# The start-up of a matmul, mask and softmax kernel: mask loaded ahead of W, fills shared among engines, TensorE run on zeros, and W four rows to a partition

## Chip, cores and metric

One core of one Trainium2 chip. The metric is device time in microseconds (us) of one execution; lower is better. "Span" is the same execution as the profile sees it, 1.7 to 2.5 us less than the measured time, by kernel. Each run carries a state. For one core, a run is called slow when it is over 1.5% above the fastest run of the same kernel, and ratios use the fast runs alone. That label matters in this case and is discussed with the result.

## The reference

```
y = scale * matmul(x, weight)          # x: 16 x 512 x 512, weight: 512 x 512, scale 0.125
y = where(mask == 1, y, -1e9)          # mask: lower triangle of 512 x 512
out = softmax(y, axis=-1)              # float32, 16 x 512 x 512
```

Traffic is 16.8 MB of x in, 16.8 MB of out, 1 MB of W and 0.26 MB of mask (only its four diagonal blocks are read).

## The kernel before

The kernel works on sixteen tiles u, each of half the rows of two batch entries, four rows of x to a partition, 1 MB in and 1 MB out. For a tile: one load, a cast to bf16 on VectorE, sixteen PE transposes, eviction of the transposes by VectorE and ScalarE, matmuls plus one "band" matmul that adds the mask, exp with row sums on ScalarE, reciprocal and scaling on VectorE, one store. Loads and stores are all issued by SyncE. Its start-up:

```python
    load(0)
    seq(nc.sync.dma_start(w_f32, weight.rearrange("(kt p) n -> p kt n", p=P)))
    seq(nc.sync.dma_start(diag_f32, diag_r))            # the mask's diagonal blocks
    for u in range(1, X_BUFS):                          # X_BUFS = 8
        load(u)
    make_identity(nc, ident_bf)
    nc.gpsimd.memset(spread, 0.0)
    # ... eight gpsimd.affine_select that build spread ...
    nc.gpsimd.memset(band[:HP, :, :, P:], MASK_NEG)
    nc.gpsimd.memset(band[HP:, :, :, :P], 0.0)
    for i in range(0, OUT_BUFS, 2):
        nc.gpsimd.memset(ots[i][:, :, HB:], 0.0)        # four wide fills
        nc.gpsimd.memset(ots[i][0:2, 0, HB:], 1.0 / N)
    cast(0); transpose(0); evict(0)
    # ... four casts of W, 128x512 each, VectorE and ScalarE in turn ...
    # ... mask to bf16 on VectorE; four matmuls spread x mask; copies into band ...
    cast(1)

    for u in range(U + 1):                              # U = 16, guards cut
        transpose(u + 1)
        cast(u + 2)
        evict(u + 1)
        multiply(u)
        normalise(u - 1); store(u - 1)
        load(u - 1 + X_BUFS)                            # only after a store is issued
```

The last line matters: after the first eight, a load is issued only behind a store. Until the first store the DMA queue holds eight x tiles, W and the mask and nothing else.

The softmax here doesn't subtract the row's maximum and nothing guards it: scores larger than these inputs give would overflow.

## Time and profile before

| | before |
|---|---|
| time, median of the first runs | 93.98 us (93.84 to 94.58, 4 runs) |
| span of the profiled run | 92.3 us (a run of 94.61 us, labelled slow) |
| bytes moved | 34.87 MB on SyncE's queue |
| first store issued | 25.63 us |
| last store issued / last byte landed | 84.57 / 91.3 us |

Two things are to be read beside the lines that the prediction shows. First, when stores are issued: the timeline of the DMA-issuing engine (start, length, engine, line, operation, what it writes and reads, count).

```profile
2.64 6.99 SPq L78 DMA_DIRECT2D xf<-in_x_dram  x7
25.63 0.61 SPq L158 DMA_DIRECT2D out_dram<-ot  x1
26.29 0.60 SPq L78 DMA_DIRECT2D xf<-in_x_dram  x1
30.77 0.60 SPq L158 DMA_DIRECT2D out_dram<-ot  x1
```

From 10 to 25.6 us nothing new enters the queue. Second, why the first store is so late: VectorE's timeline ahead of it.

```profile
5.82 2.06 DVE L83 CAST xb<-xf 128x2048 bf16<-128x2048 f32 x1 [5.82 <-DMA xf<-in_x_dram]
9.00 0.69 DVE L102 COPY xt<-pt 128x1024 bf16<-128x1024 bf16 x1 [1.13 <-PE pt L92]
9.61 3.15 DVE L193 CAST w_bf<-w_f 128x512 bf16<-128x512 f32 x2
12.68 0.61 DVE L197 TENSOR_SCALAR diag_bf<-diag_f 128x512 bf16<-128x512 f32 x1
13.96 1.70 DVE L216 CAST band<-py 64x256 bf16<-64x256 f32 x4 [0.68 <-PE py L209]
15.59 2.34 DVE L83 CAST xb<-xf 128x2048 bf16<-128x2048 f32 x2
```

A cast that takes 1.22 us later takes 2.06 here, and two W casts take 3.15 where one of them alone took 0.61. GpSimd is filling until 13.0 us. cast(1) begins near 15.6 (the first of the last row's two), 2.7 us after x(1) has landed (12.9 in the landing records).

### The profile page before, as it was taken

Reading aid. Unit: us, or ns where it says so; the run is one execution under the profiler, and the core shown is the slowest. Engines: PE = TensorE matmul, PEld = TensorE weight load, DVE = VectorE, ACT = ScalarE, POOL = GpSimd, SP = SyncE. Lnnn points to the kernel's source line nnn. Section 1 sums busy time; section 2 is a strip of 40 time slices with the busy share of each in tenths; the row PEclk is TensorE's granted clock in tenths of the full one; section 3 lists DMA queues with packets and bytes.
Section 4 is the critical chain, followed back from the end, with each engine's and each line's share of the span. In section 5 each row is a group of like instructions: output and inputs, shape, how many; then the busy total and the mean of one; then the engine's idle time right before and its main releaser. Section 6 shows DMA issues by size and latency. Waiting matters only on the chain.

```text
span 92.3 us, 1608 instructions
## 1 busy us (share of the span) xinstructions
PE 68.8 (75%) x580; PEld 48.7 (53%) x580; DVE 60.0 (65%) x119; ACT 54.4 (59%) x151; POOL 15.9 (17%) x33
## 2 busy tenths in 40 slices
PE   0005225699999999999999999999999999940000
PEld 0005100677659857956975885796598577510000
DVE  0045979950857995995999599599395977616000
ACT  5000716064868777977877788797787879650000
POOL 7999960000100010010001001000100010100000
PEclk9999999999999999999999999999999999997555
DMA  0889999999999999999999999999999999999930
GB/s 32 334 309 309 387 430 423 437 415 430 419 419 312 405 426 291 323 423 415 415 433 426 423 430 412 430 419 433 423 430 426 423 423 433 423 426 423 394 156 11
DMA packets 5670, 34.95 MB, mean 379 GB/s; under 512 B 544, under 2 KB 1056, under 8 KB 1568
## 3 DMA queue, kind: packets, MB, share of 16 engines
q1 hardware_dynamic: 5664, 34.87, 92.7%
q8 instruction: 4, 0.07, 0.3%
q14 instruction: 2, 0.02, 0.0%
HBM read 18.09 MB, written 16.78 MB: 378 GB/s over the span
## 4 chain that ended last, share of the span: by engine, by line
PE 72%; DVE 12%; DMA 5%; ACT 1%; DVEq 0%; issue 0%; ACTq 0%
PE py L116 47%; PE pt L92 17%; PE py L125 8%; DMA xf<-in_x_dram 5%; DVE xb L83 3%; DVE w_bf L193 3%; DVE band L216 2%; DVE ot L152 1%; DVE xt L102 1%; PE py L209 1%; ACT ot L135 1%; DVE diag_bf L197 1%; DVEq L263 0%; DVE rinv L150 0%; ACTq L263 0%
## 5 line engine op out<-in xcount | busy, mean ns | idle before, releaser
L116 PE MATMUL py<-w_bf,xt 128*128 128x256 bf16 (+1 forms) x256 | 51.4, 335 | 0.0
L135 ACT ACTIVATE ot<-py 128x256 f32<-128x256 f32 (+1 forms) x64 | 31.2, 493 | 9.3 <-PE py L125 9.1
L116 PEld LDWEIGHTS <-xt 128*128 128x128 bf16 x256 | 25.3, 101 | 12.6
L83 DVE CAST xb<-xf 128x2048 bf16<-128x2048 f32 x16 | 20.2, 1270 | 8.5 <-DMA xf<-in_x_dram 8.5
L92 PE MATMUL pt<-ident_bf,xb 128*128 128x128 bf16 x256 | 18.6, 231 | 9.6 <-DVE xb L83 9.6
L103 ACT COPY xt<-pt 128x1024 bf16<-128x1024 bf16 x16 | 16.2, 1012 | 15.5 <-PE pt L92 11.2
L152 DVE TENSOR_SCALAR ot<-ot,rinv 128x256 f32<-128x256 f32 (+1 forms) x64 | 23.5, 430 | 0.8
L92 PEld LDWEIGHTS <-xb 128*128 128x128 bf16 x256 | 17.0, 104 | 11.6 <-DVE xb L83 10.5
L102 DVE COPY xt<-pt 128x1024 bf16<-128x1024 bf16 x16 | 11.0, 689 | 11.3 <-PE pt L92 11.3
L125 PE MATMUL py<-band,ident_bf 128*128 128x256 bf16 x64 | 18.0, 282 | 0.0
L154 POOL MEMSET ot<- 2x256 f32 x8 | 3.6, 449 | 63.1 <-DVE ot L152 63.1
L135 ACT ACTIVATION_READ_ACCUMULATOR ot<-py 128x1 f32 x64 | 12.8, 200 | 0.0
L125 PEld LDWEIGHTS <-ident_bf 128*128 128x128 bf16 x64 | 6.5, 101 | 4.3
L150 DVE RECIPROCAL rinv<-rsum 128x4 f32<-128x4 f32 x16 | 2.7, 169 | 3.2 <-ACT ot L135 3.2
L185 POOL MEMSET ot<- 128x1024 f32 x4 | 4.6, 1185 | 0.1
L209 PE MATMUL py<-diag_bf,spread 128*128 128x512 bf16 x4 | 1.9, 620 | 3.5 <-DVE diag_bf L197 3.5
L173 POOL TENSOR_SCALAR_AFFINE_SELECT spread<-spread 128x64 bf16<-128x64 bf16 x8 | 3.2, 438 | 0.0
L193 DVE CAST w_bf<-w_f 128x512 bf16<-128x512 f32 x2 | 3.1, 1612 | 0.0
L216 ACT CAST band<-py 64x256 bf16<-64x256 f32 x4 | 1.5, 368 | 2.7 <-DVE band L216 2.5
L209 PEld LDWEIGHTS <-spread 128*128 128x128 bf16 x4 | 0.5, 136 | 4.2 <-POOL ot L186 3.7
L216 DVE CAST band<-py 64x256 bf16<-64x256 f32 x4 | 1.7, 416 | 0.7 <-PE py L209 0.7
L103 ACT ACT_TABLE_LOAD x1 | 1.3, 1283 | 0.7 <-PEq L249 0.7
(12 smaller groups left out, 6.8 us busy)
## 6 DMA issues: line engine op xcount, KB each, us to landing
xf<-in_x_dram SPq DMA_DIRECT2D x16, 1024.0 KB, 14.1
out_dram<-ot SPq DMA_DIRECT2D x16, 1024.0 KB, 11.0
w_f<-in_weight_dram SPq DMA_DIRECT2D x1, 1024.0 KB, 7.6
diag_f<-in_mask_dram SPq DMA_DIRECT2D x1, 256.0 KB, 8.3
```

Source lines behind the costliest of these rows:

```text
L83: seq(nc.vector.tensor_copy(xb, st_x.pop(u)))
L92: nc.tensor.transpose(st_pt[u][kt // 2][:, kt % 2, t], xb[:, t, kt * P : (kt + 1) * P], ident_bf,)
L102: seq(nc.vector.tensor_copy(xt[:, 0:2], pt[0]))
L103: seq(nc.scalar.copy(xt[:, 2:4], pt[1]))
L116: nc.tensor.matmul(py[:, :NC], lhsT=xt[:, kt, t], rhs=w_bf[:, kt, :NC], start=(kt == 0), stop=(kt == KT - 1),)
L125: nc.tensor.matmul(py[:, h * HB : NC], lhsT=ident_bf, rhs=band[:, h, t], start=False, stop=True, skip_group_check=True,)
L135: nc.scalar.activation(out=ot[:, t, :NC], in_=py[:, :NC], func=AF.Exp, bias=0.0, scale=float(scale), accum_out=rsum[:, t : t + 1],)
L152: seq(nc.vector.tensor_scalar_mul(ot[:, t, :NC], ot[:, t, :NC], rinv[:, t : t + 1]))
L154: seq(nc.gpsimd.memset(ot[0:2, 0, :HB], 1.0 / N))
L185: nc.gpsimd.memset(ots[i][:, :, HB:], 0.0)
L193: seq(nc.vector.tensor_copy(w_bf[:, kt], w_f32[:, kt]))
L216: seq(copy(band[half, :, t, g * P : (g + 1) * P], src[half, :, g]))
```

## The change

The intent is a shorter start-up. Cut to its core:

```diff
-    seq(nc.sync.dma_start(w_f32, weight.rearrange("(kt p) n -> p kt n", p=P)))
     seq(nc.sync.dma_start(diag_f32, diag_r))
+    seq(nc.sync.dma_start(w_f32, weight.rearrange("(p kt) n -> p kt n", kt=KT)))
@@ transpose(u)
-                        xb[:, t, kt * P : (kt + 1) * P],
+                        xb[:, t].rearrange("p (k kt) -> p kt k", kt=KT)[:, kt],
@@ ahead of make_identity
+    nc.vector.memset(zeros, 0.0)
+    idle = psum_y.tile([P, N], FP32, name="py")
+    for _ in range(WARM):                       # WARM = 12
+        seq(nc.tensor.matmul(idle, lhsT=zeros[:, :P], rhs=zeros, start=True, stop=True))
@@ fills
-    nc.gpsimd.memset(spread, 0.0)               # and eight affine_select, cut
-        nc.gpsimd.memset(ots[i][:, :, HB:], 0.0)
+        nc.vector.memset(ots[i][:, :, HB:], 0.0)
+    # spread: four nc.scalar.copy out of ident_bf, cut
@@ order on the engines
     cast(0)
-    transpose(0); evict(0); four casts of W; mask to bf16; band
+    mask to bf16; transpose(0); evict(0); band; two casts of W (128x1024 each)
     cast(1)
```

The pseudo-lines of the last part stand for the moved blocks. W's rows now lie four to a partition, in runs of 8 KB, so the transposes take every fourth column of x, a step of four bf16 elements.

## The prediction

> **What bounds the kernel now.** I read the page first, then the chain of waits, the windows view, the waits of the DMA-issuing queue and the timeline of VectorE. The page offers TensorE as the bound: it holds 72% of the chain that ended last. In time order that chain shows no TensorE gap from 16.85 to 81.9 us. But the page's slices show the DMA engines at 90% or more from the second slice almost to the end, so I asked for stretches. The windows view (columns: stretch and its length; busy time and count of PE, PEld, DVE, ACT, POOL; granted clock; DMA share; GB/s):
>
> ```profile
> 2.20:5.20 3.00, 0.00 (x0) 0.00 (x0) 0.00 (x0) 0.00 (x0) 3.00 (x8) 1.00 0.92 353
> 5.20:10.20 5.00, 1.89 (x16) 1.73 (x17) 3.26 (x3) 0.34 (x1) 4.89 (x7) 1.00 0.87 308
> 10.20:27.00 16.80, 12.02 (x73) 7.71 (x73) 12.02 (x18) 8.60 (x22) 3.25 (x5) 1.00 1.01 425
> ...
> 28.00:32.00 4.00, 4.00 (x50) 3.54 (x48) 3.71 (x8) 3.27 (x12) 0.00 (x0) 1.00 0.99 350
> ...
> 35.00:39.00 4.00, 4.00 (x49) 3.53 (x48) 2.85 (x8) 3.45 (x12) 0.00 (x0) 1.00 0.90 285
> 39.00:85.00 46.00, 42.90 (x375) 29.91 (x372) 35.22 (x79) 34.35 (x100) 2.69 (x6) 0.99 1.01 425
> ...
> 88.50:91.30 2.80, 0.00 (x0) 0.00 (x0) 0.00 (x0) 0.00 (x0) 0.00 (x0) 0.50 0.10 44
> ```
>
> Look at the last column. 425 GB/s is the ceiling: both long stretches sit on it. The queue's 34.87 MB at 425 GB/s need 82.0 us, and the first packet moves at 2.2 us, so no order of the compute can land the last byte before about 84.2 us. It lands near 91.3. The 7 us between are the stretches below 425, each costing length x (1 - rate/425): 0.5 us in 2.2-5.2, 1.4 in 5.2-10.2, 0.7 in 28-32, 1.3 in 35-39, some 0.4 in 85-88.5, and 2.5 in the tail after 88.5, where 44 GB/s is one or two of 16 engines finishing late.
>
> Why the rate falls: I counted bytes issued against bytes moved in the packet records. The eight loads, W and the mask run out at 27 us, when 0.07 MB is left. The first store is issued at 25.63 and needs about 1.6 us to begin, the second at 30.77, when little is left again. From 41 us the backlog is 1.5 to 5 MB, and it is down to 0.14 MB at 86. So the DMA queue bounds the kernel, and compute matters only where it feeds stores too late: around 27-32 us and at the very end. VectorE's timeline shows the other direction, loads arriving late for compute:
>
> ```profile
> 66.79 1.23 DVE L83 CAST xb<-xf 128x2048 bf16<-128x2048 f32 x1 [1.43 <-DMA xf<-in_x_dram]
> ...
> 71.64 1.23 DVE L83 CAST xb<-xf 128x2048 bf16<-128x2048 f32 x1 [1.23 <-DMA xf<-in_x_dram]
> ```
>
> The bracket is idle time before the row and what ended it. The last two x tiles are already late for VectorE, so moving the whole compute chain earlier cannot move its end by the same amount.
>
> **What the Trainium skill says.** "DMA: Bandwidth & Descriptors", Specifications, puts the fabric ceiling at 435 GB/s; the 425 above agrees within 3%. "TensorE: Matmul & The Clock Gate", Part 1, says that matmuls start at half clock until about 3.4 us of sustained work. The trace agrees in form: sixteen transposes take 1.89 us at 16.85 but 0.89 at 22.99. The granted-clock column shows 1.00 in both places, so here I trust durations. "SBUF — State Buffer", the cacheline note in the port-swizzle section (Door 1), says steps up to 8 bf16 elements read at full rate; the new transposes step by 4. No run yet shows a strided weight load. The same page, Who interferes with whom, says a GpSimd instruction and a two-port VectorE one exclude each other; the trace agrees: the first cast, beside GpSimd fills, took 2.06 us, the median of its kind is 1.22.
>
> **The change, part by part.**
>
> 1. W at four rows to a partition: 512 packets of 2 KB become 128 of 8 KB. Packet records give medians of 84 and 309 ns: 512 x 84 / 16 = 2.69 us against 128 x 309 / 16 = 2.47. It saves 0.2 us of DMA time, and I grant 0.3 more because W's packets started with a gap (DMA share 0.58 at 5-6 us).
>
> 2. Fills. GpSimd loses 0.53 + 3.2 us for the spread matrix and 4.6 for the wide fills (4 x 1185 ns). VectorE takes the wide fills; it has no such row yet, so I use GpSimd's 1.2 us each, 4.8 in all, inside its idle 5.8 us before x(0) lands. ScalarE builds spread in four small copies, also while idle. None is on the path. GpSimd should be done before the first cast, which then takes 1.22 instead of 2.06: 0.8 us earlier.
>
> 3. Mask before W. Before, W's cast (3.1 us on VectorE, one piece slowed to 2.6 by GpSimd) stood ahead of the mask's 0.6 us, and the band matmuls waited for it until 13.34. Now: cast(0) 5.8 to 7.0, mask landed near 7.1 and converted by 7.8, eviction 0.7, four band copies of 0.42 us by about 10.5. W lands about 9.5; its cast (twice 0.61 us, nobody interfering) ends near 11.8. Then cast(1) waits for x(1), which landed at 12.9 in the records and should at 12.4-12.6. It ends near 13.8 instead of 16.80. Transposes(1) start **2.9 us earlier**, and that is set by a load.
>
> 4. Zeros on TensorE: twelve matmuls of 512 columns at 427 ns (half clock, the page's name) make 5.1 us from about 1.1, off the path. They may warm the clock for transposes(0). TensorE then idles from about 9.5 to 13.8, long enough for the clock to drop again; I give it one chance in two. If it stays warm, multiply(0) takes 2.2 us instead of 4.25 and the chain gains another 2 to 3 us.
>
> 5. Strided transposes: same 256 instructions. I expect the same 0.89 us for sixteen.
>
> So the first store goes out at 21-23.2 us instead of 25.63, the second at 26.3-28.5 instead of 30.77: both before the queue runs dry. That fills 28-32 (0.7 us) and the starvation of 85-88.5 (0.4), since the last store, issued at 84.6 before, would be ready at 82 or earlier and then waits in the queue. The dip at 35-39 fell with 2 MB queued, so I cannot call it starvation; I count half, 0.65. The late engines at the end fell behind in the same two dips (the slowest landed with the others until 25.3, then lost 4.7 us to 42); I count 1.0 of the tail's 2.5. With 0.5 for W: 0.7 + 0.4 + 0.65 + 1.0 + 0.5 = **3.25 us**, giving 93.99 - 3.25 = **90.7 us**.
>
> **The rivals.**
>
> - *The chain is TensorE's, so its whole start-up gain shows.* For it: 72% of the chain. Then 3 to 6 us come off: 88 to 91. Against it: the floor of 84.2 us for the last byte plus its fixed ends (1 us from landing to the end of span, 2.3 between span and measured time, both from this trace) is 87.5, and the late x tiles push compute back.
> - *All is hidden by the DMA.* If the dips are the memory's doing and not starvation, only W's 0.5 us and the ending remain: about 93. The dip at 35-39 with a full queue speaks for this; the empty queue at 27 and the clean 425 GB/s once backlog exists speak against.
> - *Strided weight loads are slow.* If sixteen transposes cost 1.78 us instead of 0.89, TensorE needs 0.89 x 16 = 14 us more, a pair of tiles 9.6 us instead of 7.86, and it becomes the bound: 97 us or more. The cacheline note speaks against it; no trace does. I give 3%.
>
> **Range and chances.** Recovering everything but the mask's small packets and one late engine gives 89.4; recovering only W and the ends about 92.5. My range is 89.4 to 92.3. Faster by over 2% means below 92.1: all dips would have to be someone else's to miss that. I say 0.84; within 2% 0.15; slower 0.01.
>
> **What would show each step.** Right: the DMA column at 425 GB/s from 10 us to the end with no dip at 28-32; the first store near 22 us; transposes(1) near 13.9 behind a wait of cast(1) on x(1); more waits of casts on x tiles in the second half; a last store that waits several us in the queue; the sixteen transposes still 0.89 us. Wrong: a dip that returns at the first stores although bytes are queued would make the memory the cause and the time 92 to 93; transposes over 1.3 us for sixteen would mean the stride costs; a TensorE gap in mid-kernel with the DMA share under 0.9 would mean a new wait. A tail with one engine 2 to 3 us late, as now, would put me 1 us too low.

## The result, and the profile after

| | before | after |
|---|---|---|
| median of the first runs | 93.98 us (4 runs) | 90.89 us (90.86 to 90.90, 4 runs) |
| ratio, first runs | 1 | 0.966, 95% interval 0.962 to 0.970 |
| ratio, later job, fast runs | 1 | 0.988, interval 0.982 to 0.994 |
| span of the profiled run | 92.3 us (run of 94.61 us, slow) | 89.1 us (run of 90.89 us) |
| first / second store issued | 25.63 / 30.77 | 23.05 / 28.19 |
| last store issued / last byte landed | 84.57 / 91.3 | 81.99 / 88.1 |

A ratio here is the one on record: mean time of one kernel's fast runs over that of the other's fast runs of the same rounds, so it is not quite the ratio of the medians. The two ratios differ, and the reason is the kernel before. In 98 later runs it spread from 91.6 to 94.8 us with a median of 93.9: 43 runs lay under 93.5, 55 above, and 59 carry the label slow. Its fast runs average 92.4, and against those the recorded gain is 1.2%: at the line of 2% that verdict is "unclear". Against a typical run, or against the four first ones, it is over 3%; those four were labelled by themselves, and all lie among the times that the later jobs label slow. The granted TensorE clock does not explain the slow runs: 21 of the 59 stand at 0.953 to 0.961, below every fast run, but the other 38 at 0.967 to 0.974, as the fast ones do. The changed kernel's ten runs all lie between 90.86 and 91.35. So the change does two things: it lowers the best time a little (91.6 to 90.9 us), and it removes a spread of 3 us. A difference that only the slow runs of before showed would not be safe to explain; the run `late` below shows the same times and the same dips in runs that carry the label fast.

The windows view of after, with the columns as in the prediction:

```profile
2.20:5.20 3.00, 3.00 (x9) 1.06 (x7) 2.51 (x4) 0.94 (x4) 1.80 (x4) 1.00 0.93 348
5.20:10.20 5.00, 3.41 (x24) 1.41 (x21) 3.62 (x8) 1.79 (x4) 0.30 (x1) 1.00 0.81 307
10.20:27.00 16.80, 12.65 (x97) 9.37 (x99) 9.62 (x17) 9.08 (x22) 0.45 (x1) 0.80 1.02 425
...
28.00:32.00 4.00, 3.95 (x34) 2.55 (x33) 3.96 (x9) 3.08 (x9) 0.45 (x1) 1.00 1.02 430
35.00:39.00 4.00, 3.95 (x37) 2.85 (x36) 3.96 (x10) 3.21 (x12) 0.45 (x1) 1.00 1.02 424
39.00:85.00 46.00, 40.05 (x349) 28.49 (x352) 32.75 (x73) 32.52 (x96) 2.24 (x5) 0.96 1.01 425
85.00:88.10 3.10, 0.00 (x0) 0.00 (x0) 0.00 (x0) 0.00 (x0) 0.00 (x0) 0.50 0.44 185
```

Both dips are gone: 28-32 went from 350 to 430 GB/s, 35-39 from 285 to 424. Look at the DMA share as well, the number ahead of the rate. In the dips of before it stood at 0.99 and 0.90, and in one microsecond of the first dip even above 1 (a packet counts whole in the stretch where it begins):

```profile
29.00:30.00 1.00, 1.00 (x11) 0.90 (x10) 0.96 (x4) 1.00 (x3) 0.00 (x0) 1.00 1.14 270
```

So the engines were not idle in the dips; their packets took longer. By the packet records 79 of the 465 packets of 8 KB that began in 28-39 us took over 450 ns, with a median of 606 instead of 309. Together the packets of this stretch took 1.7 us of all 16 engines more than at 309 ns each, of the 2.0 us lost. In after it was one packet of 570.

The first 10 us did not improve. The ending lost less. With the same arithmetic as the prediction, length x (1 - rate/425), the books close:

| stretch | lost before, us | lost after, us | gain |
|---|---|---|---|
| 2.2 to 10.2 | 1.9 | 1.9 | 0.0 |
| 28 to 32 | 0.7 | 0.0 | 0.7 |
| 35 to 39 | 1.3 | 0.0 | 1.3 |
| 85 to the last byte | 2.9 | 1.75 | 1.15 |
| sum | 6.8 | 3.65 | 3.15 |

The span fell by 92.3 - 89.1 = 3.2 us. Two cautions belong to these books. They describe a slow run of before, 94.61 us, not the median of 93.98 and not a fast run. And the measured time of that run fell by more than its span, 94.61 - 90.89 = 3.7 us: about 0.5 us of the gain lies outside the profiled span. Measured time less span is 2.2 to 2.5 us in every run on record of the kernels whose spread and wide fills are on GpSimd (before, `before_x10`, `fills_pool`) and 1.7 to 1.9 us in every run of the others. So this half microsecond goes with the shared fills; what it is made of is not shown.

The start-up on VectorE, from its timeline in after:

```profile
5.79 1.23 DVE L85 CAST xb<-xf 128x2048 bf16<-128x2048 f32 x1 [0.36 <-DMA xf<-in_x_dram]
8.04 0.43 DVE L194 TENSOR_SCALAR diag_bf<-diag_f 128x512 bf16<-128x512 f32 x1 [1.02 <-DMA diag_f<-in_mask_dram]
...
10.54 0.69 DVE L216 CAST w_bf<-w_f 128x1024 bf16<-128x1024 f32 x1 [0.15 <-DMA w_f<-in_weight_dram]
13.02 1.23 DVE L85 CAST xb<-xf 128x2048 bf16<-128x2048 f32 x1 [1.79 <-DMA xf<-in_x_dram]
```

The first two stores, from the timeline of the issuing queue:

```profile
23.05 0.61 SPq L160 DMA_DIRECT2D out_dram<-ot  x1
28.19 0.60 SPq L160 DMA_DIRECT2D out_dram<-ot  x1
```

Every VectorE row shown now waits for a load (see the brackets) and none for GpSimd. cast(1) begins 0.03 us after x(1) has landed (12.99). That wait replaced 2.7 us of other work, as the prediction's third part said, and the chain behind it moved by 25.63 - 23.05 = 2.58 us.

TensorE's timeline of after, the transposes of tile 1 and of tile 2:

```profile
14.30 1.89 PE L94 MATMUL pt<-ident_bf,xb 128*128 128x128 bf16 x16 [4.76 <-DVE xb L85]
20.24 1.06 PE L94 MATMUL pt<-ident_bf,xb 128*128 128x128 bf16 x16
```

After 4.76 us without work the clock was down again: sixteen transposes took 1.89 us, as before, and the clock records of this run show half speed from 13.39 to 20.22 us (hence 0.80 in the clock column of 10.2 to 27). Strided or packed, they take the same time.

### The profile page after: what moved, and what is told of

The parts are those of the page before. It is cut to its first block, busy times and chain, and to the rows that moved or that the text cites. A ratio compares the mean times of both kernels' runs of the same rounds, so it can differ in the third digit from the quotient of the medians.

```text
span 89.1 us, 1610 instructions
## 1 busy us (share of the span) xinstructions
PE 72.0 (81%) x584; PEld 49.4 (56%) x592; DVE 60.5 (68%) x123; ACT 55.3 (62%) x154; POOL 7.3 (8%) x20
## 3 DMA queue, kind: packets, MB, share of 16 engines
q1 hardware_dynamic: 5280, 34.87, 93.9%
## 4 chain that ended last, share of the span: by engine, by line
PE 73%; DMA 12%; DVE 3%; SPq 2%; issue 1%; ACT 1%; DVEq 0%; ACTq 0%
PE py L118 48%; PE pt L94 16%; DMA xf<-in_x_dram 12%; PE py L127 8%; DVE ot L154 1%; DVE xb L85 1%; SPq L80 1%; ACT ot L137 1%; SPq L164 1%; SPq L165 1%; DVEq L264 0%; DVE rinv L152 0%; ACTq L264 0%
## 5 line engine op out<-in xcount | busy, mean ns | idle before, releaser
L85 DVE CAST xb<-xf 128x2048 bf16<-128x2048 f32 x16 | 19.5, 1220 | 5.9 <-DMA xf<-in_x_dram 5.9
L94 PE MATMUL pt<-ident_bf,xb 128*128 128x128 bf16 x256 | 17.8, 225 | 5.3 <-DVE xb L85 5.3
L156 POOL MEMSET ot<- 2x256 f32 x8 | 3.6, 448 | 67.7 <-DVE ot L154 67.7
L173 PE MATMUL py<-zeros 128*128 128x512 bf16 x12 | 5.3, 632 | 1.2 <-DVE zeros L170 1.2
L179 DVE MEMSET ot<- 128x1024 f32 x4 | 3.6, 912 | 0.6 <-issue 0.6
L173 PEld LDWEIGHTS <-zeros 128*128 128x128 bf16 x12 | 1.6, 144 | 3.9 <-issue 2.8
L208 PE MATMUL py<-diag_bf,spread 128*128 128x512 bf16 x4 | 1.0, 377 | 0.4 <-DVE diag_bf L194 0.4
L180 POOL MEMSET ot<- 2x256 f32 x4 | 1.2, 302 | 1.5 <-DVE ot L179 1.4
## 6 DMA issues: line engine op xcount, KB each, us to landing
xf<-in_x_dram SPq DMA_DIRECT2D x16, 1024.0 KB, 13.9
```

Source lines behind the costliest of these rows:

```text
L85: seq(nc.vector.tensor_copy(xb, st_x.pop(u)))
L94: nc.tensor.transpose(st_pt[u][kt // 2][:, kt % 2, t], xb[:, t].rearrange("p (k kt) -> p kt k", kt=KT)[:, kt], ident_bf,)
L156: seq(nc.gpsimd.memset(ot[0:2, 0, :HB], 1.0 / N))
L173: seq(nc.tensor.matmul(idle, lhsT=zeros[:, :P], rhs=zeros, start=True, stop=True))
L179: nc.vector.memset(ots[i][:, :, HB:], 0.0)
```

## The experiments

All were run in three chip jobs, each kernel timed beside the kernel before on the same chip. `after_again` is the yardstick of the first. It is the only yardstick, so kernels of different jobs are compared by their medians, with the yardstick's spread of 0.5 us in mind. The third job ran on another chip than the first two; the fast runs of before average 92.3 to 92.4 us in all three.

### The yardstick

> The changed kernel once more, unedited, as the yardstick for the other runs of this chip job. Both theories (queue-bound and TensorE-chain) expect 90.9 us, ratio to before 0.966.

Measured: 91.04 us (90.86 to 91.35, 6 runs), all labelled fast, ratio 0.988. Its profiled run took 90.88 us, as in the first job, but its stores were issued earlier:

```profile
22.12 0.61 SPq L160 DMA_DIRECT2D out_dram<-ot  x1
81.06 0.54 SPq L160 DMA_DIRECT2D out_dram<-ot  x1
```

The first store went out 0.93 us earlier and so did the last (81.06 against 81.99), because the clock records rise to full speed at 18.3 instead of 20.2 us. The last byte landed at 88.10 instead of 88.08. The program is the same, so this is the cleanest evidence that in the changed kernel the compute chain no longer sets the end.

### Zeros on TensorE taken out (`no_warm`)

```diff
-WARM = 12
+WARM = 0
```

> The changed kernel without the twelve matmuls on zeros. My theory: the clock drops again before transposes(1) anyway (their sixteen took 1.89 us in the changed kernel, the slow size), and only transposes(0) get slower (1.89 instead of 1.09 us), which is hidden because cast(1) waits for x(1) until 13.0 us. So 90.9 us, within 0.2 us of the yardstick. Rival (the zeros are worth something): 0.5 to 1 us slower, 91.4 to 91.9.

Measured: 91.00 us (90.80 to 91.21, 6 runs). TensorE's timeline of this kernel:

```profile
7.30 1.90 PE L94 MATMUL pt<-ident_bf,xb 128*128 128x128 bf16 x16 [7.30 <-DVE xb L85]
...
14.26 1.90 PE L94 MATMUL pt<-ident_bf,xb 128*128 128x128 bf16 x16 [3.36 <-DVE xb L85]
...
19.01 1.06 PE L94 MATMUL pt<-ident_bf,xb 128*128 128x128 bf16 x16
```

The issuing queue's timeline has the first store:

```profile
21.82 0.61 SPq L160 DMA_DIRECT2D out_dram<-ot  x1
```

The zeros shorten the first transposes (1.09 against 1.90 us) and the four band matmuls (1.0 against 1.9), which are both hidden behind the wait for x(1). In this execution the clock rose earlier, at 17.7 instead of 20.2 us, so the transposes of tile 2 and the first store came 1.2 us sooner than in the changed kernel. The time did not move. The last store was issued at 80.76, 1.23 us earlier, and landed at 88.24 instead of 88.08. So compute is not what bounds the changed kernel: a first store at 21.8 us is worth no more than one at 23.05.

### W in 2 KB rows again (`w_2k`)

```diff
-weight.rearrange("(p kt) n -> p kt n", kt=KT)
+weight.rearrange("(kt p) n -> p kt n", p=P)
-xb[:, t].rearrange("p (k kt) -> p kt k", kt=KT)[:, kt]
+xb[:, t, kt * P : (kt + 1) * P]
```

> The changed kernel with W back in 2 KB rows and packed transposes. My theory: 2.69 instead of 2.47 us of DMA time, so x(1) and everything after it lands 0.2 us later, up to 0.5 if many small packets also open gaps: 91.1 to 91.4 us. Transposes stay 0.89 us for sixteen on the fast clock. Rival (descriptor shape is a main part of the gain): 92 us or more.

Measured: 91.21 us (91.11 to 91.28, 6 runs), 0.17 over the yardstick. That alone would be within the yardstick's spread, but x(1) landed at 13.25 us instead of 12.99. The packets' arithmetic, 0.22 us, is about right; the extra 0.3 that the prediction granted for gaps is not there.

### The kernel before once more (`before_again`)

> The kernel before, unedited, to get a profile of one of its fast executions: in the first job its 27 runs fell into two groups, 91.6 to 93.0 and 93.8 to 94.6 us, while the changed kernel's six all lay within 90.9 to 91.4. Theory starvation: the queue runs dry at 27 us in every run and what is random is how far single DMA engines fall behind in the dips; a fast run still shows 350 GB/s or less at 28-32 but not the deep dip at 35-39. Rival (a disturbance from outside): fast runs have no dip at all.

Measured: 94.08 us (91.97 to 94.76, 22 runs). The profile that came back was again of a slow run, so what a fast run of before looks like inside stays open. The dips are there a second time, 363 GB/s at 28-32 and 313 at 35-39, at the same places but of other depth.

### Ten x buffers in the kernel before (`before_x10`)

```diff
-X_BUFS = 8
+X_BUFS = 10
```

> The kernel before with ten x buffers instead of eight, so that 2 MB more are queued when the first store comes; its compute starts no earlier. Theory starvation: no dip between 27 and 39 us, x(14) and x(15) on time, the second group of slow runs gone; the end is then the compute chain's, last store issued near 84.6 and landed about 5 us later: 91.5 to 92.3 us in nearly all runs. Rival (the memory or the first stores make the dips): still 91.6 to 94.6 in two groups.

Measured: 91.81 us (91.55 to 92.18, 15 runs), no slow run; 0.993 of the fast runs of before, so the best time hardly moves. The windows view:

```profile
28.00:32.00 4.00, 4.00 (x40) 3.06 (x39) 3.96 (x10) 3.53 (x11) 0.12 (x1) 1.00 1.01 420
32.00:35.00 3.00, 3.00 (x26) 1.83 (x24) 1.89 (x5) 2.14 (x7) 0.33 (x1) 1.00 1.01 423
35.00:39.00 4.00, 4.00 (x48) 3.42 (x45) 3.96 (x8) 3.27 (x12) 0.00 (x0) 1.00 1.01 428
82.00:85.00 3.00, 0.00 (x0) 0.00 (x0) 1.41 (x4) 0.00 (x0) 0.00 (x0) 1.00 0.78 330
```

Without any of the change, with 2 MB more in the queue, both dips and the slow group are gone. The dip at 35-39, which fell with 2 MB queued and which the prediction could not place, therefore points to the same trigger as the first one. The first store came at 24.50 us here, since TensorE's clock rose earlier in this execution; the buffers are not the only difference in time. A first store at 24.5 us with eight buffers was not tried, so for this one trace the earlier store stays a rival; that none of 15 runs was slow, at granted clocks from 0.967 to 0.986, speaks for the buffers. About 0.5 us of the 0.8 that this kernel stays behind the changed one lies outside the span. The last row shows the new limit: with its last store at 83.44 us the compute chain is now too late for the end, and the queue is short of work at 82-85.

### The changed kernel with its compute held back (`late`)

```diff
+    delay = const.tile([P, 2 * N], FP32, name="delay")
@@ ahead of cast(1)
+    for _ in range(4):
+        seq(nc.vector.memset(delay, 0.0))
     cast(1)
```

> The changed kernel with four dummy fills of 128x1024 on VectorE (about 4.3 us, of which 1.8 fill an idle wait) ahead of cast(1), so that its first store comes near 25.5 us as in the kernel before; all else is as changed. Theory starvation: the dips at 28-39 us come back, and so does the spread: 91.4 to 94.5 us, median above 92. Rival (the gain comes from something else in the change, such as W's packets or the fills): 91 us, single group.

Measured: 94.08 us (93.60 to 94.51, 6 runs), all labelled fast. First store at 25.34, second at 30.47 us. The windows view:

```profile
28.00:32.00 4.00, 4.00 (x47) 3.43 (x45) 3.96 (x8) 3.27 (x12) 0.00 (x0) 1.00 1.01 399
32.00:35.00 3.00, 3.00 (x17) 1.50 (x16) 2.67 (x7) 2.43 (x7) 0.45 (x1) 1.00 1.00 366
35.00:39.00 4.00, 4.00 (x53) 3.72 (x51) 3.14 (x7) 3.37 (x12) 0.00 (x0) 1.00 0.93 315
```

This is the decisive run. Everything of the change is in it, and 2.3 us of delay to the first store cost 3 us and brought the dips back. It is not that each microsecond of the chain counts: in `no_warm` the first store moved by 1.2 us and the time by nothing. Not all of the 3 us are the dips, though. By the rates they cost 1.7 us (28 to 39 us), and the ending 1.0 us more than in the changed kernel. That part a late chain may cost by itself: the last store was issued at 84.28, and in `before_x10`, with no dips, a last store took 4.9 us to land.

When the first store begins, the old queue has just been drained: 0.84 MB were left at 25.0 us, about 2 us of work, and a store needs 1.6 us from its issue to its first packet. That timing is the trigger. But inside the dips the queue was not empty. Counted from the issue of each transfer, never less than 0.8 MB was still to be moved from 28 to 32 us and never less than 2.3 MB from 34 to 39, and 52 packets of 8 KB took over 450 ns, much as in before. How a queue that has almost run dry makes later packets slow is not shown. The spread that I expected did not come: all six runs lie where the kernel before has its slow ones. What decides in the kernel before whether a run is one of the fast ones is not shown.

### W ahead of the mask again (`w_then_mask`)

The loads of W and mask change places, and VectorE's and ScalarE's work on W goes ahead of the mask's conversion; all else stays.

> The changed kernel with W ahead of the mask again (W still in 8 KB rows), its conversion ahead of the mask's. The changed kernel's mask packets directly after x(0) left the engines 40 to 50% busy for 2 us; with W's 8 KB packets ahead the mask's should be ready in the queue by their turn (in the kernel before they lost only about 0.35 us after W). Theory queue-bound: x(1) lands 0.5 to 0.8 us sooner and the end with it: 90.2 to 90.6 us. Rival (mask first is what makes the gain): slower than the changed kernel, 92 or more.

Measured: 91.13 us (90.97 to 91.16, 6 runs). Both theories fell. First store at 22.50. The mask's packets were slow here too: 232 of 512 bytes in the stretch where the mask ran alone, 0.12 MB per us, against 244 in the changed kernel. x(1) landed at 13.01 instead of 12.99. So the mask costs the engines about a microsecond in both of these places (in the kernel before, behind W's 2 KB packets, about 0.4 us by the DMA shares of 8-10 us). With the fills shared, the order of mask and W makes no difference to the time.

### Shared fills alone (`fills_only`)

The kernel before, with the wide fills on VectorE and spread copied by ScalarE.

> The kernel before with one part of the change alone: the wide fills on VectorE and spread copied by ScalarE; order of loads and conversions, 2 KB rows of W, no zeros on TensorE. My theory: GpSimd's fills made the kernel before late (first cast 2.06 us instead of 1.23, one W cast 2.6 instead of 0.6, together 2.8 us ahead of cast(1)); without them cast(1) begins when x(1) lands, near 13.0 us, the first store goes out near 23.3, the queue never runs dry: 91.1 to 91.4 us in one group. Rival (mask ahead of W is what brings the start forward): 92 us or more, in two groups.

Measured: 91.09 us (91.00 to 91.19, 6 runs). VectorE's timeline:

```profile
6.07 1.23 DVE L83 CAST xb<-xf 128x2048 bf16<-128x2048 f32 x1 [0.91 <-DMA xf<-in_x_dram]
...
9.44 0.76 DVE L190 CAST w_bf<-w_f 128x512 bf16<-128x512 f32 x2 [0.32 <-DMA w_f<-in_weight_dram]
...
13.32 1.21 DVE L83 CAST xb<-xf 128x2048 bf16<-128x2048 f32 x1
```

The first store went out at 22.20 us. The two W casts take 0.76 us together instead of 3.15, the first cast 1.23 instead of 2.06. One part alone gives the whole gain, within the yardstick's spread.

### All but the shared fills (`fills_pool`)

The changed kernel with spread and the wide fills back on GpSimd.

> The changed kernel with spread and the wide fills back on GpSimd; all else as changed. If the new order of mask and W is enough by itself, cast(1) begins by 13.7 us, the first store goes out by 23.8 and the time is 91.0 to 91.4. If GpSimd's fills block VectorE's casts as they did before, cast(1) begins at 14.5 or later, the first store after 24.5, and the slow group with its dips returns: over 92.

Measured: 91.39 us (91.28 to 91.57, 6 runs). cast(1) began at 12.98 us and the first store went out at 21.90. The slow first cast (1.80 us) and the slow mask conversion (1.06 instead of 0.43) still fit ahead of x(1), but only just: GpSimd was filling until 13.28 us, W's cast took 1.00 us instead of 0.69, and VectorE was ready 0.20 us before x(1) landed. So the rest of the change is also sufficient without the shared fills; which part of it (the loads' order, the order on the engines, W in two casts) was not taken apart. The 0.35 us over the yardstick lie outside the span: the spans, 89.0 to 89.3 us, are those of the changed kernel, and measured time less span is 2.3 us instead of 1.8, as in the kernel before.

### The mask on a second queue (`mask_actq`, `mask_act_late`)

```diff
-    seq(nc.sync.dma_start(diag_f32, diag_r))
+    nc.scalar.dma_start(diag_f32, diag_r)          # mask_actq: at the start
+    seq(nc.scalar.dma_start(diag_f32, diag_r))     # mask_act_late: behind ScalarE's copies of spread in the program
```

> The changed kernel with the mask's load issued from ScalarE's queue instead of SyncE's. In the changed kernel the DMA engines moved only about 0.12 MB per us while the mask's 512-byte packets went through (some 3.2 to 5.5 us after the first packet is counted), because nothing else was in their queue's turn. Theory queue-bound: another queue lets x(0) and W fill those slots; x(1) lands about 1.0 us earlier, the whole transfer and compute shift with it: 89.9 us. Rival (the mask's own packets are what is slow and take the engines with them wherever they are issued): 90.9 us.

> The mask issued from ScalarE's queue after its four copies, near 3.2 us, when x(0) is mostly moved, so that its small packets share the engines with W's large ones. In the first try with that queue the 16 engines finished x(0) between 3.8 and 6.4 us, and the slowest stayed behind to the end. Theory queue-bound: x(1) lands near 12.0 instead of 13.0, end about 0.8 us sooner: 90.2 us. Rival (the skew between engines comes with any second queue): 90.9 to 91.6.

Measured: 91.66 us (91.38 to 93.94, 22 runs, three of them slow) and 98.26 us (97.70 to 99.02, 6 runs). Both expectations failed, in different ways. In the first, the mask's packets went ahead of x(0): 187 GB/s in 2.2-5.2 us, and by the landing records the 16 engines finished the mask between 3.8 and 6.4 us and x(0) only between 6.7 and 8.9, where the changed kernel's finish x(0) between 5.3 and 5.8. (The next expectation takes the mask's landings for those of x(0).) The engines were then 2.1 us apart instead of 0.5, and still were at x(1). The mean gained a little, the slowest engine lost, and x(1) is there only when the slowest has it: 13.85 instead of 12.99 us. The three slow runs show a lower granted clock (0.878 against 0.91 to 0.94) and were not looked into. In the second, the issue came at 2.2 us, with x(0) and W already queued. VectorE's timeline:

```profile
18.23 0.43 DVE L194 TENSOR_SCALAR diag_bf<-diag_f 128x512 bf16<-128x512 f32 x1 [10.95 <-DMA diag_f<-in_mask_dram]
```

In each microsecond from 5 to 13 after the first packet the records count 41 to 59 mask packets and 34 to 48 of 8 KB. By these counts the two queues took turns, about one packet for one, so the small mask was stretched over some 12 us. The first store was issued at 31.4 us, and the windows view of this kernel shows the empty queue in its pure form:

```profile
27.00:28.00 1.00, 1.00 (x7) 0.67 (x6) 0.00 (x0) 0.41 (x3) 0.00 (x0) 0.50 0.00 0
28.00:29.00 1.00, 1.00 (x13) 0.85 (x12) 0.00 (x0) 0.63 (x3) 0.00 (x0) 0.80 0.00 0
```

From 32 us the queue moved again, and the same slow packets followed: 43 over 450 ns in 34-36 us and 41 in 40-44. That supports the drained queue as the trigger.

### Earliest compute and fullest queue (`warm2_x10_late`)

The previous kernel with eighteen more zero matmuls ahead of cast(1) and ten x buffers.

> The previous kernel with eighteen more matmuls on zeros between the band and transposes(1), to hold TensorE's clock, and ten x buffers: compute as early as it can be, queue as full as it can be. Theory queue-bound: compute ends a further 1 to 3 us earlier and this is worth at most 0.2 us beyond the previous kernel: 90.0 to 90.2. Rival (TensorE's chain still sets the end): 88 to 89.

Measured: 97.64 us (96.69 to 98.26, 6 runs, one of them slow). It inherits the late mask (VectorE waits 10.85 us for it), so it says nothing about the question it was made for. No kernel that was tried beats the changed one by more than the yardstick's spread.

## Why the prediction was right, by its own steps

- **The bound.** Right that the DMA queue is the bound. In after the rate stands at 425 GB/s from 10 us to 85, and `no_warm`, `late` and `before_x10` show from three sides that the first store's time counts only through the queue: at 21.8 to 23.05 us it makes no difference (90.9 to 91.4 us in six kernels, not in the order of their first stores), at 25.34 it costs 3 us. The rival that the whole start-up gain shows is refuted by `no_warm` and `after_again`; the rival that nothing shows, by `late`.
- **Starvation as the reason for the dips.** Right in the trigger, not shown in the mechanism. The prediction's count evidently leaves a store out until 1.6 us after its issue. Counted from the issue, at least 0.9 MB was queued in the first dip of before and at least 2.3 MB in the second, with the engines busy and packets at 606 ns. Its own sign of being wrong, a dip although bytes are queued, was thus met in before and again in `late`. The memory by itself is not the cause either, since the same stores and loads ran at 420 to 430 GB/s in the changed kernel and in `before_x10`, where from 26 to 39 us at least 1.7 and 3.3 MB were queued.
- **W's rows and gaps: 0.5 us.** Mis-sized. `w_2k` gives about 0.2; the first 10 us as a whole lost 1.9 us before and after. The gap that I saw ahead of W simply moved to the mask.
- **Fills.** Right in kind and nearly in size: the first cast took 1.23 us (1.22 predicted). VectorE's own fill took 0.91 us, not 1.2. What the prediction did not say is that this part is sufficient alone, and that the rest is sufficient too (`fills_only`, `fills_pool`): either one brings cast(1) to within 0.3 us of the landing of x(1). Nor did it see the half microsecond outside the span that goes with this part; it carried 2.3 us between span and measured time over as fixed, and 1.8 were measured.
- **Mask ahead of W.** The chain was right (cast(1) waits for x(1); 13.02 us against about 12.5), and transposes(1) began at 14.30 instead of 13.9. But `w_then_mask` shows that the position of the mask is not what does it.
- **Zeros.** Right to give them nothing (the twelve took 5.3 us together, 5.1 predicted). The clock fell back, the less lucky half of the even chance.
- **Strided transposes.** Right: 1.06 us for sixteen, first to last end, against 1.08 before. The weight loads are recorded at 113 ns instead of 98, but their pace is hidden beside the matmuls.
- **The dip at 35-39: 0.65 us, half of it.** Mis-sized: all 1.3 came back, and `before_x10`, where it is gone, points to the same trigger as for the first dip, although bytes were queued by then. How, the runs do not show.
- **The ending: 0.4 + 1.0 us.** 1.15 measured. But not for the reason given: in the profiled run the last store did not wait longer in the queue (landed 6.1 us after its issue, 6.7 before), and the rate is still a little short at 85-86 us (369 GB/s). Where the clock rose earlier it did wait, 7.0 us in `after_again` and 7.5 in `no_warm`, and gained nothing by it.
- **More late x tiles in the second half.** Wrong in the profiled run: casts waited 1.7 us for the last two tiles, 2.7 before, because x(15) landed 3.2 us sooner and compute moved by 2.6. In `after_again` they waited 2.9.

The sum, 3.25 us, met the 3.15 of the span's books with two terms too large (W, the ending) and one too small (the dip at 35-39). That the time was met as well, 90.7 against 90.89, is partly luck. The sum came from the profile of a 94.61 us run and was taken from a median of 93.99, and the 0.5 us outside the span, which nobody foresaw, made up for most of that difference. It was luck too that the four first runs of before were all slow ones: 59 of 98 later runs are, so the chance of four out of four is about one in eight, an estimate from that share. Against a fast run of before the gain is about 1.3 us.

## What to carry to other kernels

When a page shows an engine with no gap and the DMA engines nearly full as well, read the rate by stretches and add up bytes issued against bytes moved: here the stretches below the ceiling that began where the queue had almost run dry are what a faster start-up bought back, and little beyond them. Before rearranging a start-up, find the time by which the first store must be issued to keep the queue fed; one more prefetch buffer or two may buy most of what five careful edits buy (91.8 us here, from one number). In this case scatter between executions of an unchanged kernel, most of it at the same clock, led to the queue. And look up which run the profile is of: here it was a slow one.

## What the Trainium skill lacked or had wrong

- "DMA: Bandwidth & Descriptors", Specifications, gives 512 bytes as the size from which a transfer runs at line rate. The mask's 512-byte packets, alone in the queue, moved 0.12 MB per us with the engines 46 to 50% busy, in the changed kernel and in `w_then_mask` (244 and 232 packets per us for all 16 engines); 8 KB packets moved 0.43.
- The same page, "Issuing engines are not separate DMA queues", says that issuing on several engines only saves issue time. For the order of arrival that does not hold here: the mask, issued at 2.2 us on the second queue, landed at 18.2 instead of 8.0 us, and the time was 98.3 instead of 91.0. "Queues, rings and completion order" on that page does tell of the turns between queues, of some 9 to 17 descriptors each. The counts here, about one 512-byte packet to one of 8 KB, show turns of about equal length, not how long one is.
- The same Specifications table lists 358 GB/s per core for HBM, half of a stack's rate. For a core alone that is too low: in the changed kernel it held 425 GB/s for 75 us (10 to 85). "HBM Reference", Specifications, has it right for a core alone.
- No page was found that tells that one DMA engine's lag lasts to the end when the queue never empties. In the changed kernel the slowest engine finished x(6) at 26.8 us, 1.4 after the next, in the same microseconds in which a 16 KB instruction fetch took 1.1 us (at 23.9 us; at 27.2 in the kernel before, with x(7) late by 1.5), and the last store was still 2.0 us apart between the first engine and the last. That the fetch is the cause was not tested.
- "SBUF — State Buffer", the cacheline note, calls a step of four bf16 elements free. The matmul pace agrees; the recorded weight load grew from 98 to 113 ns.
- No page was found that tells of two things above: packets of 8 KB at 606 ns and more instead of 309 within some 11 us after the queue had almost run dry, with the engines busy; and 2.3 us between measured time and profiled span with the fills on GpSimd, 1.8 us without.
